# Score matmuls of the second block: from three passes of 64 rows for each head to one of 128 rows and one of 64

## The chip, the cores and the metric

The kernel runs on one core of a Trainium2 chip, as one launch. The metric is the device time of that launch in microseconds (us). A core has a matrix engine (TensorE, in the rows PE, its weight loads PEld), VectorE (DVE), ScalarE (ACT), GpSimd (POOL) and a queue engine (SP), which run side by side and wait for one another by semaphores.

## The reference

The reference is a net of two blocks of two layers each, over 512 tokens of width 1024, all in float32. The first block (RWKV-7, latent attention, a convolution, attention into a memory) is not touched. The second block is, for each layer:

```python
u = rmsnorm(h, attn_norm[l])
rq, rk, rv, rg, dq, dk, dv = split(u @ w_in[l])
# retention, 4 heads, q and k of 64: scores with a decay, causal
s = einsum('bnchd,bnshd->bnhcs', q, k) * decay
ret = silu(rg) * rmsnorm(retention(rq, rk, rv), ret_norm[l])
# differential attention, 4 heads, two q and two k of 64 each
s = einsum('bqhjd,bkhjd->bhjqk', qb, kb) * scale - slope * dist   # causal
p = softmax(s)
a = p[:, :, 0] - lam * p[:, :, 1]
dif = rmsnorm(a @ v, diff_norm[l]) * (1 - lam_init)
h = h + concat([ret, dif]) @ w_out[l]
h = h + (silu(u2 @ w_gate[l]) * (u2 @ w_up[l])) @ w_down[l]       # u2 = rmsnorm(h, ffn_norm[l])
```

What counts here are the two products of q and k, whose inner dimension is 64.

## The kernel before

Float32 products are made out of three passes in a rounded format (F32R): an operand x is split into hi, its rounding, and lo = x - hi, and a.b is taken as hi.hi + hi.lo + lo.hi, summed in PSUM. `hilo` (L259) makes the two parts: a ScalarE cast for hi (L260), a VectorE subtraction for lo (L243 by way of `tt`). Weights go the same way, from a raw tile `wr` to `wh` and `wl`. A projection (`proj`, L351) is 24 matmuls of 512 columns into a PSUM tile `pmm` (lines 289, 290 and 295), of which there are three; score tiles are `pat`, also three; `prw` two. SBUF tiles of the second block are K4 (18 of 4 KB per partition) and K2 (32 of 2 KB); all show as `K` in the rows.

Queries and keys come out of the projection transposed: 128 partitions by 512 tokens. The 128 partitions are two heads of 64 in retention, and in diff attention the two q (or k) of one head. `mm3_pair` (L274) makes the scores for both halves: for each of the three passes it issues one matmul on partitions 0 to 63 and one on 64 to 127, each into its own PSUM tile, with 64 rows of the array each. All its matmuls have the line L279.

`retention(l)` (L1416) projects rq and rk of two pairs of heads (p = 0, 1), multiplies each by a table of decays (L1427) and splits it (L1428). Its `scores(p)` goes over key blocks j in the groups (0), (1, 3), (2): the scores of keys j against the queries from 128 j on, so 512, 384, 128 and 256 columns; VectorE multiplies each by a mask out of PSUM (L1448), and `hilo` splits that. `diff(l)` (L1482) makes for each of four heads a `query(h)` (dq and dk projections, operands hi and lo in one K4 tile for q and one for k), then `scores(h)`: for query blocks i = 0 to 3 `attn_scores2` (L1026) makes the scores against 128 (i + 1) keys for both halves, and `attn_row` (L1035) reads them out of PSUM (L1037, bias and row maximum), then exponential, sum and so on. The order of emission is query(0), scores(0), query(1), scores(1), query(2), out(0), and so on: `out(h)` transposes the weights and multiplies by the values.

The order on each engine is set when the program is built: a planner takes the operation with the best priority (about the order of emission, shifted by `prio`) out of those that it reckons to be ready. On the chip each engine then follows its list in order. So a matmul whose operand is late holds up all that stand behind it on TensorE.

Of the kernel before, what the change touches and what calls it, by code (L numbers as in the profile page):

```python
# [12 lines left out]
F32 = mybir.dt.float32  # L13
F32R = mybir.dt.float32r
I32 = mybir.dt.int32
AF = mybir.ActivationFunctionType
ALU = mybir.AluOpType
# [193 lines left out]
class Net:  # L211
# [59 lines left out]
        mm(out, ah, bl, start=False, stop=False)  # L271
        mm(out, al, bh, start=False, stop=stop)  # L272

    def mm3_pair(self, ops):  # L274

        mm = self.nc.tensor.matmul
        for i in range(3):
            for out, ah, al, bh, bl in ops:
                mm(out, (ah, ah, al)[i], (bh, bl, bh)[i], start=(i == 0), stop=(i == 2))  # L279

    def mmset(self, out, terms, start=True, stop=True):

# [743 lines left out]
    def attn_scores2(self, Svs, q, k, i, bias):  # L1026

        with self.prio("attn_scores"):
            n = (i + 1) * 128
            pss = [self.PS("at") for _ in range(2)]  # L1030
            self.mm3_pair([(pss[j][:, 0:n], q[r, 0, ts(i, 128)], q[r, 1, ts(i, 128)], k[r, 0, 0:n], k[r, 1, 0:n])
                           for j, r in enumerate((slice(0, 64), slice(64, 128)))])
            return [self.attn_row(Svs[j], pss[j], n, bias, 1.0) for j in range(2)]

    def attn_row(self, Sv, ps, n, bias, sc):  # L1035
# [380 lines left out]
    def retention(self, l):  # L1416
        nc = self.nc
        tri = [self.T("K2") for _ in range(2)]
        for i in range(2):
            nc.gpsimd.dma_start(out=tri[i], in_=self.a["cstb"][8 + i])  # L1420
        qk = []
        for p in range(2):
            for i, nm in enumerate(("rq", "rk")):
                tab = self.T("K2")
                nc.gpsimd.dma_start(out=tab, in_=self.a["cstb"][2 * i + p])
                ps = self.proj(self.bchunk(l, nm, p) if p else self.early[i], cut=0 if p else 256)
                self.tt(tab, ps, tab, ALU.mult)  # L1427
                qk.append(self.split(tab))  # L1428
                yield

        def scores(p):

            (qh, ql), (kh, kl) = qk[2 * p:2 * p + 2]
            rows = [slice(64 * hh, 64 * hh + 64) for hh in range(2)]
            HL = [(self.T("K4", dt=F32R), self.T("K4", dt=F32R), self.T("K2", dt=F32R)) for _ in range(2)]
            ST = [[None] * 4 for _ in range(2)]
            for gi, grp in enumerate(((0,), (1, 3), (2,))):
                pss = [self.PS("at") for _ in range(2)]
                o = 0
                for j in grp:  # L1440
                    n = 512 - 128 * j
                    self.mm3_pair([(pss[hh][:, o:o + n], kh[r, ts(j, 128)], kl[r, ts(j, 128)], qh[r, 128 * j:512],
                                    ql[r, 128 * j:512]) for hh, r in enumerate(rows)])
                    o += n
                for hh in range(2):
                    H, Lo, M = HL[hh]
                    t = self.T("K2")
                    self.tt(t[:, 0:o], pss[hh][:, 0:o], tri[gi % 2][:, 0:o], ALU.mult)  # L1448
                    a, b = (H[:, ts(gi, 512)], Lo[:, ts(gi, 512)]) if gi < 2 else (M[:, 0:256], M[:, 256:512])
                    self.hilo(a, b, t[:, 0:o])  # L1450
                    i = 0
                    for j in grp:
                        n = 512 - 128 * j
                        ST[hh][j] = (a[:, i:i + n], b[:, i:i + n])
                        i += n
            return ST

        STs = scores(0)
        yield
        for h in range(4):  # L1460
            gt = self.silu2(self.proj(self.bchunk(l, "rg", h)))
            yield
            if h == 0:
                STs += scores(1)
            yield
            ST = STs[h]
            ps = self.PS("rw")
            for j in range(4):
                self.mm3(ps[:, 128 * j:512], self.vals[j][0][:, ts(h, 128)], self.vals[j][1][:, ts(h, 128)],
                         ST[j][0], ST[j][1], j == 0, j == 3)  # L1470
            y = self.rms_head(ps, self.bpar[:, l:l + 1])
            self.stt(y, y, 0.5, gt, ALU.mult, ALU.mult)
            self.dump("ret", y, h)
            self.mix_in(y)
            yield
# [6 lines left out]
    def diff(self, l):  # L1482
        nc = self.nc
        lam_init = 0.8 - 0.6 * math.exp(-0.3 * l)
        lt = self.T("K2", [128, 4, 64])
        nc.sync.dma_start(out=lt, in_=self.a["lam"][l].unsqueeze(0).broadcast_to([128, 4, 64]))
        st = self.tiny(4)
        for i in range(2):
            nc.vector.tensor_tensor_reduce(lt[:, 2 * i, :], lt[:, 2 * i, :], lt[:, 2 * i + 1, :], 1.0, 0.0,
                                           op0=ALU.mult, op1=ALU.add, accum_out=st[:, i:i + 1])  # L1490
        self.act(st[:, 0:2], st[:, 0:2], AF.Exp)
        self.tt(st[:, 2:3], st[:, 1:2], st[:, 0:1], ALU.subtract)
        nlam = self.tiny(2)
        self.tsc(nlam[:, 0:1], st[:, 2:3], -lam_init, ALU.add)
        self.tsc(nlam[:, 1:2], self.bpar[:, 2 + l:3 + l], 1.0 - lam_init, ALU.mult)
        yield
        def query(h):
            al = self.T("K2")
            nc.gpsimd.dma_start(out=al, in_=self.a["cstb"][4 + h])
            ps = self.proj(self.bchunk(l, "dq", h))  # L1500
            q, k = self.T("K4", [128, 2, 512], F32R), self.T("K4", [128, 2, 512], F32R)
            self.act(q[:, 0, :], ps, AF.Copy, scale=0.125)
            self.stt(q[:, 1, :], ps, 0.125, q[:, 0, :].bitcast(F32), ALU.mult, ALU.subtract)
            yield
            self.hilo(k[:, 0, :], k[:, 1, :], self.proj(self.bchunk(l, "dk", h)))
            yield
            qs[h] = al, q, k

        def scores(h):
            al, q, k = qs.pop(h)  # L1510
            Sj = [self.score_tiles() for _ in range(2)]
            for i in range(4):
                m0, m1 = self.attn_scores2([P[i] for P in Sj], q, k, i, al)
                self.tt(m1[:, 3:4], m1[:, 3:4], nlam[:, 0:1], ALU.mult)
                self.ptsc(Sj[1][i], Sj[1][i], m1[:, 3:4], ALU.mult, 1.0, ALU.mult)
                self.stt(Sj[0][i], Sj[0][i], m0[:, 3:4], Sj[1][i], ALU.mult, ALU.add)
            return Sj[0]

        def out(h, P):
            PT = self.attn_T(P)  # L1520
            ps = self.PS("rw")
            for j in range(4):
                self.mm3(ps[:, 128 * j:512], self.dvals[j][0][:, ts(h, 128)], self.dvals[j][1][:, ts(h, 128)],
                         PT[j][0], PT[j][1], j == 0, j == 3)
            y = self.rms_head(ps, nlam[:, 1:2])
            self.dump("dif", y, h)
            self.mix_in(y)

        qs = {}
        yield from query(0)  # L1530
        prev = None
        for h in range(4):
            P = scores(h)
            yield
            if h < 3:
                yield from query(h + 1)
            if prev:
                out(h - 1, prev)
                yield
            prev = P  # L1540
        out(3, prev)
        yield
# [165 lines left out]
```

## Time and profile before

| | |
|---|---|
| median of 3 runs | 2924.97 us (2923.43 to 2925.59) |
| the profiled execution's own time | 2923.72 us |
| its span, first to last instruction | 2921.9 us |
| mean granted clock of TensorE | 0.987 |
| TensorE / VectorE / ScalarE / GpSimd busy, share of the span | 97% / 60% / 39% / 10% |

A row of the timeline merges neighbouring instructions of one line on one engine: its first number is the start from the beginning of the span, the second how long the merged run lasts. Matmuls are pipelined, so that the next one starts before the one before it has ended; what a matmul costs TensorE is seen from start to start. In the rows `64*128 64x512` means that 64 rows and 128 columns of the array are used and that 512 columns stream through, and a bracket at the end gives the idle time before and what ended it.

### The profile page before, as it was taken

What the parts mean: (1) busy time and instruction counts of PE and PEld (TensorE: products, weight loads), DVE (VectorE), ACT (ScalarE), POOL (GpSimd) and SP (SyncE); (2) the same over time, 40 slices, a digit from 0 to 9 for tenths busy, and PEclk for the clock granted to TensorE, in tenths of its full rate; (3) what the DMA queues carried; (4) which work ended last, traced back from release to release, by engine and by line L of the source; (5) the groups of instructions that cost most, each with busy time, mean ns of one, the idle gap of its engine ahead of it and who ended that gap; (6) DMA issues with size and microseconds to landing.
All of it is one profiled execution on the core that took longest, in us unless ns stands there. A gap on an engine that the chain in (4) does not pass through costs nothing. (4 is left out here: it accounts for less than half of the span.)

```text
span 2921.9 us, 40859 instructions
## 1 busy us (share of the span) xinstructions
PE 2825.3 (97%) x15172; PEld 2305.8 (79%) x15172; DVE 1741.8 (60%) x3499; ACT 1154.0 (39%) x2230; POOL 298.3 (10%) x451
## 2 busy tenths in 40 slices
PE   8999989999999999989899999999999999999998
PEld 7777867777787878777687778788888887788888
DVE  7969467576669696485676645554433546544423
ACT  5445443343434455433433334433323335433322
POOL 0011021111001011111210101100000101100000
PEclk9999999999999999999999999999999999999999
DMA  5222223123342222231242232223333222233332
GB/s 172 73 76 67 79 76 93 44 81 117 106 141 80 74 67 73 78 87 57 74 136 66 87 98 81 73 84 97 105 97 106 88 66 81 73 94 101 101 94 91
DMA packets 134535, 258.09 MB, mean 88 GB/s; under 512 B 15936, under 2 KB 19776, under 8 KB 134336
## 3 DMA queue, kind: packets, MB, share of 16 engines
q1 hardware_dynamic: 128896, 239.22, 26.8%
q0 software_dynamic: 5440, 16.26, 2.1%
q8 instruction: 119, 1.95, 0.3%
q14 instruction: 80, 0.66, 0.1%
HBM read 248.60 MB, written 6.82 MB: 87 GB/s over the span
## 5 line engine op out<-in xcount | busy, mean ns | idle before, releaser
L243 DVE TENSOR_TENSOR wl<-wr,wh 128x512 fp32r<-128x512 f32 x792 | 541.1, 686 | 724.4 <-ACT wh L260 393.5
L289 PE MATMUL pmm<-xh,wh 128*128 128x512 f32 x2272 | 883.6, 391 | 1.5 <-DVE K L243 1.5
L290 PE MATMUL pmm<-xl,wh 128*128 128x512 f32 x2272 | 878.6, 389 | 0.0
L260 ACT CAST wh<-wr 128x512 fp32r<-128x512 f32 x792 | 487.5, 616 | 848.3 <-PE pmm L290 528.6
L295 PE MATMUL pmm<-xh,wl 128*128 128x512 f32 x2272 | 578.6, 391 | 0.0
L289 PEld LDWEIGHTS pmm<-xh,wh 128*128 128x128 f32 x2272 | 429.1, 189 | 88.1 <-PE pmm L295 2.3
L290 PEld LDWEIGHTS pmm<-xl,wh 128*128 128x128 f32 x2272 | 428.8, 189 | 85.1 <-issue 0.8
L295 PEld LDWEIGHTS pmm<-xh,wl 128*128 128x128 f32 x2272 | 420.0, 190 | 85.8 <-issue 2.8
L246 DVE SCALAR_TENSOR_TENSOR cacc<-hp,par,cacc 128x512 f32<-128x512 f32 x240 | 183.1, 763 | 4.1
L243 DVE TENSOR_TENSOR K<-K,K 128x512 fp32r<-128x512 f32 (+14 forms) x261 | 151.1, 583 | 57.4 <-ACT K L260 49.9
L260 ACT CAST K<-K 128x512 fp32r<-128x512 f32 (+1 forms) x122 | 73.5, 606 | 186.2 <-DVE K L246 129.8
L289 PE MATMUL pmm<-K,wh 128*128 128x512 f32 (+1 forms) x352 | 135.1, 392 | 5.1 <-DVE big L246 4.0
L254 POOL TENSOR_SCALAR K<-K,tiny 128x256 f32<-128x256 f32 (+3 forms) x128 | 80.4, 635 | 505.3 <-DVE tiny L250 221.1
L290 PE MATMUL pmm<-K,wh 128*128 128x512 f32 (+1 forms) x352 | 131.2, 380 | 0.0
L422 PE MATMUL pat<-cst,K 128*128 128x128 f32 (+2 forms) x656 | 102.2, 277 | 21.0 <-DVE K L246 13.0
L240 ACT ACTIVATE K<-pmm 128x512 f32<-128x512 f32 (+1 forms) x118 | 70.6, 598 | 108.6 <-PE pmm L295 108.5
L257 POOL TENSOR_TENSOR tiny<-tiny,negh 128x4 f32<-128x4 f32 (+2 forms) x54 | 66.0, 1222 | 454.6 <-DVE tiny L251 280.2
L422 PEld LDWEIGHTS pat<-cst,K 128*128 128x128 f32 (+2 forms) x656 | 76.8, 141 | 35.5 <-DVE K L246 10.6
L270 PE MATMUL pmm<-wh,K 128*128 128x512 f32 x260 | 103.8, 402 | 0.0
L272 PE MATMUL pmm<-wh,K 128*128 128x512 f32 x260 | 103.6, 398 | 0.0
L271 PE MATMUL pmm<-wl,K 128*128 128x512 f32 x260 | 103.6, 398 | 0.0
L246 DVE SCALAR_TENSOR_TENSOR K<-K,pmm 128x512 f32<-128x512 f32 x130 | 88.4, 680 | 5.9 <-ACT K L240 5.9
(335 smaller groups left out, 4132.6 us busy)
## 6 DMA issues: line engine op xcount, KB each, us to landing
wr<-in_wA SPq DMA_DIRECT2D x316, 256.0 KB, 2.7
wr<-in_wgu SPq DMA_DIRECT2D x176, 256.0 KB, 2.9
wr<-in_wo SPq DMA_DIRECT2D x64, 256.0 KB, 2.8
wr<-in_wout SPq DMA_DIRECT2D x64, 256.0 KB, 2.9
wr<-in_wB SPq DMA_DIRECT2D x64, 256.0 KB, 2.8
wr<-in_wdA SPq DMA_DIRECT2D x44, 256.0 KB, 2.8
wr<-in_wdB SPq DMA_DIRECT2D x44, 256.0 KB, 2.7
K<-in_cstb POOLq DMA_DIRECT2D x20, 256.0 KB, 3.3
```

Source lines behind the costliest of these rows:

```text
L240: return self.nc.scalar.activation(out, in_, func, bias=bias, scale=scale, **kw)
L243: return self.nc.vector.tensor_tensor(out=out, in0=a, in1=b, op=op)
L246: return self.nc.vector.scalar_tensor_tensor(out=out, in0=a, scalar=s, in1=b, op0=op0, op1=op1)
L254: return self.nc.gpsimd.tensor_scalar(out=out, in0=a, scalar1=s1, scalar2=s2, op0=op0, op1=op1)
L260: self.nc.scalar.copy(h, src)
L270: mm(out, ah, bh, start=start, stop=False)
L271: mm(out, ah, bl, start=False, stop=False)
L272: mm(out, al, bh, start=False, stop=stop)
L289: mm(out, ah, bh, start=start and i == 0, stop=False)
L290: mm(out, ah, bl, start=False, stop=False)
L295: mm(out, al, bh, start=False, stop=stop and i == n - 1)
L422: self.nc.tensor.transpose(out, in_, self.ident[b:b + k, :k] if k == 128 else self.ident[b:b + k, b:b + k])
```

## The change

Of the two operands of a score product, one is stacked and the other doubled. For a half (64 partitions), the stacked operand holds hi in its own 64 partitions and lo in the other 64 of one tile; the doubled operand holds hi in both. One pass of 128 rows then gives hi.hi + lo.hi. A second pass, of 64 rows, multiplies the stacked tile's hi part by the doubled operand's lo, which has a tile of its own. So each half has two passes instead of three, and they are issued half by half: full, half, full, half. In retention q is doubled and k is stacked, in diff q is stacked and k doubled. The parts are made by operations over 64 partitions each. Other users of `hilo` and `mm3` stay as they are.

```diff
-    def mm3_pair(self, ops):
-
-        mm = self.nc.tensor.matmul
-        for i in range(3):
-            for out, ah, al, bh, bl in ops:
-                mm(out, (ah, ah, al)[i], (bh, bl, bh)[i], start=(i == 0), stop=(i == 2))
+    def stacked(self, a, b, src, scale=None):
+
+        for t, r, o in ((a, slice(0, 64), slice(64, 128)), (b, slice(64, 128), slice(0, 64))):
+            if scale is None:
+                self.nc.scalar.copy(t[r, :], src[r, :])
+                self.tt(t[o, :], src[r, :], t[r, :].bitcast(F32), ALU.subtract)
+            else:
+                self.act(t[r, :], src[r, :], AF.Copy, scale=scale)
+                self.stt(t[o, :], src[r, :], scale, t[r, :].bitcast(F32), ALU.mult, ALU.subtract)
+        return a, b
+
+    def doubled(self, a, b, lo, src):
+
+        for t, r, o in ((a, slice(0, 64), slice(64, 128)), (b, slice(64, 128), slice(0, 64))):
+            self.nc.scalar.copy(t[r, :], src[r, :])
+            self.nc.scalar.copy(t[o, :], src[r, :])
+            self.tt(lo[r, :], src[r, :], t[r, :].bitcast(F32), ALU.subtract)
+        return a, b, lo
+
+    def mm_half(self, out, half, st, db, q, n0, n1):
+
+        r = slice(64 * half, 64 * half + 64)
+        self.nc.tensor.matmul(out, st[half][:, q], db[half][:, n0:n1], start=True, stop=False)
+        self.nc.tensor.matmul(out, st[half][r, q], db[2][r, n0:n1], start=False, stop=True)
...
-            self.mm3_pair([(pss[j][:, 0:n], q[r, 0, ts(i, 128)], q[r, 1, ts(i, 128)], k[r, 0, 0:n], k[r, 1, 0:n])
-                           for j, r in enumerate((slice(0, 64), slice(64, 128)))])
+            for j in range(2):
+                self.mm_half(pss[j][:, 0:n], j, q, k, ts(i, 128), 0, n)
...
-                qk.append(self.split(tab))
+                t = [self.T("K2", dt=F32R) for _ in range(2 + (i == 0))]
+                qk.append(self.stacked(*t, tab) if i else self.doubled(*t, tab))
...
-                    self.mm3_pair([(pss[hh][:, o:o + n], kh[r, ts(j, 128)], kl[r, ts(j, 128)], qh[r, 128 * j:512],
-                                    ql[r, 128 * j:512]) for hh, r in enumerate(rows)])
+                    for hh in range(2):
+                        self.mm_half(pss[hh][:, o:o + n], hh, ks, qd, ts(j, 128), 128 * j, 512)
...
-            self.act(q[:, 0, :], ps, AF.Copy, scale=0.125)
-            self.stt(q[:, 1, :], ps, 0.125, q[:, 0, :].bitcast(F32), ALU.mult, ALU.subtract)
-            yield
-            self.hilo(k[:, 0, :], k[:, 1, :], self.proj(self.bchunk(l, "dk", h)))
+            q = self.stacked(q[:, 0, :], q[:, 1, :], ps, 0.125)
+            yield
+            k = self.doubled(k[:, 0, :], k[:, 1, :], self.T("K2", dt=F32R), self.proj(self.bchunk(l, "dk", h)))
```

## Rows read from the trace of the kernel before

**Rows 1.** The page: TensorE's busy time, share of the span, instructions.

```profile
PE 2825.3 (97%) x15172; PEld 2305.8 (79%) x15172; DVE 1741.8 (60%) x3499; ACT 1154.0 (39%) x2230; POOL 298.3 (10%) x451
```

**Rows 2.** Busy time by stage, a stretch with a diff head; ends with granted clock, DMA.

```profile
1791.00:1807.00 16.00, 15.78 (x78) 12.61 (x76) 10.94 (x41) 7.75 (x19) 0.00 (x0) 1.00 0.34 106
```

**Rows 3.** Timeline of TensorE, 0.05 us at the first retention scores.

```profile
1695.94 0.39 PE L295 MATMUL pmm<-xh,wl 128*128 128x512 f32 x1
1696.26 0.51 PE L279 MATMUL pat<-K,K 64*128 64x512 f32 x2
```

**Rows 4.** Timeline of TensorE, a single score matmul among those of 128 rows.

```profile
1711.09 0.50 PE L279 MATMUL pat<-K,K 64*128 64x512 f32 x1
1711.51 0.50 PE L290 MATMUL pmm<-K,xh 128*128 128x512 f32 x1
1711.85 0.40 PE L289 MATMUL pmm<-K,xh 128*128 128x512 f32 x1
1712.08 0.40 PE L290 MATMUL pmm<-K,xh 128*128 128x512 f32 x1
```

**Rows 5.** Timeline of TensorE, matmuls of 384, 256 and 128 columns.

```profile
1835.66 0.33 PE L270 MATMUL prw<-K,K 128*128 128x384 f32 x1
...
1836.19 0.28 PE L270 MATMUL prw<-K,K 128*128 128x256 f32 x1
...
1836.54 0.22 PE L270 MATMUL prw<-K,K 128*128 128x128 f32 x1
...
1836.71 0.27 PE L272 MATMUL prw<-K,K 128*128 128x128 f32 x1
1836.92 0.95 PE L279 MATMUL pat<-K,K 64*128 64x128 f32 x9
```

**Rows 6.** Timeline of TensorE, runs of score matmuls of the first layer.

```profile
1696.26 1.79 PE L279 MATMUL pat<-K,K 64*128 64x512 f32 x12
1699.10 1.81 PE L279 MATMUL pat<-K,K 64*128 64x384 f32 x12 [1.04 <-DVE K L243]
1701.58 1.61 PE L279 MATMUL pat<-K,K 64*128 64x512 f32 x3 [0.68 <-DVE K L243]
1703.12 1.65 PE L289 MATMUL pmm<-K,xh 128*128 128x512 f32 x3
...
1734.65 1.07 PE L279 MATMUL pat<-K,K 64*128 64x512 f32 x7
...
1736.76 1.81 PE L279 MATMUL pat<-K,K 64*128 64x384 f32 x12
...
1803.15 4.19 PE L279 MATMUL pat<-K,K 64*128 64x128 f32 x24
1807.27 0.50 PE L289 MATMUL pmm<-xh,wh 128*128 128x512 f32 x1
...
1842.12 2.83 PE L279 MATMUL pat<-K,K 64*128 64x256 f32 x15
```

**Rows 7.** Granted clock by stretch: length, TensorE busy, clock, DMA share, GB/s.

```profile
1701.30:1708.10 6.80, 6.52 (x15) 0.50 0.39 117
2322.50:2329.30 6.80, 6.47 (x15) 0.50 0.34 114
```

**Rows 8.** Timeline of TensorE, projection at the lower clock.

```profile
1704.57 0.63 PE L290 MATMUL pmm<-K,xh 128*128 128x512 f32 x1
1704.99 0.63 PE L289 MATMUL pmm<-K,xh 128*128 128x512 f32 x1
```

**Rows 9.** Timeline of VectorE at the first retention scores.

```profile
1697.75 0.69 DVE L243 TENSOR_TENSOR K<-K,K 128x512 fp32r<-128x512 f32 x1 [0.69 <-ACT K L260]
1698.36 1.88 DVE L243 TENSOR_TENSOR K<-pat,K 128x512 f32<-128x512 f32 x3
```

**Rows 10.** Groups by shape, operations over 64 partitions: busy time, mean ns.

```profile
L260 ACT CAST K<-pmm 64x512 fp32r<-64x512 f32 x16 | 9.3, 581 | 0.2
L243 DVE TENSOR_TENSOR K<-pmm,K 64x512 fp32r<-64x512 f32 x16 | 10.9, 684 | 0.8 <-ACT K L260 0.7
```

More of the change, by code (lines that the diff above doesn't have):

```diff
@@ L1427, in retention @@
                 self.tt(tab, ps, tab, ALU.mult)
-                qk.append(self.split(tab))
+                t = [self.T("K2", dt=F32R) for _ in range(2 + (i == 0))]
+                qk.append(self.stacked(*t, tab) if i else self.doubled(*t, tab))
                 yield
         def scores(p):
-            (qh, ql), (kh, kl) = qk[2 * p:2 * p + 2]
-            rows = [slice(64 * hh, 64 * hh + 64) for hh in range(2)]
+            qd, ks = qk[2 * p:2 * p + 2]
             HL = [(self.T("K4", dt=F32R), self.T("K4", dt=F32R), self.T("K2", dt=F32R)) for _ in range(2)]
```

## The prediction, made before the changed kernel was run

> **What bounds the kernel now.** I read the page first: TensorE holds 97% of the span [rows 1], so a time on TensorE counts in full unless it takes the place of a wait. Busy time there is the union of pipelined matmuls and hides small gaps, so the sums below go by start times from the timeline of TensorE alone. The table of stages shows what the change's other engines have left around a head of diff attention [rows 2]: VectorE is busy 10.94 of 16 us, ScalarE 7.75. Neither is the bound; VectorE has the less to spare.
>
> The question is then what the score matmuls of line 279 cost TensorE. Three things are to be seen.
>
> First, the two heads of a pair already share the array. Two matmuls of 64 rows and 512 columns start within 0.05 us of each other and together last 0.51 us [rows 3]; one alone lasts 0.50 us [rows 4]. So three passes over two heads can cost about three passes, not six.
>
> Second, going between 64 and 128 rows costs time. In the steady run the matmuls of 512 columns start 0.23 us apart (1711.85 to 1712.08). Around the single score matmul at 1711.09 the next starts come after 0.42 and 0.34 us [rows 4]; a matmul of 64 rows comes 0.32 us after the start of 128 rows before it (1695.94 to 1696.26) [rows 3]. So one matmul of 64 rows among those of 128 takes 0.32 + 0.42 + 0.34 = 1.08 us where three steady starts take 0.69: 0.40 us for two switches, 0.20 each. About 0.09 of that comes before the new matmul starts, and about 0.11 after, where its weights have to be loaded before it streams (0.50 us long against 0.39 to 0.40).
>
> Third, the pairs run far from their best, since they wait. A head of diff attention has 24 matmuls, which hold TensorE from 1803.15 to 1807.27, 4.12 us [rows 6]; twelve perfect pairs would need half of that. In retention there are idle stretches of 1.04 and 0.68 us ended by VectorE [rows 6], and then a granted clock of 0.50, the 1.2 GHz level, from 1701.3 to 1708.1, and the same in the second layer from 2322.5 [rows 7].
>
> **The old cost.** Diff, one layer: two heads run as 24 in a row, 4.12 us each; the other two run as 9 and 15, rows of 0.95 and 2.83 us [rows 5, 6], whose last 0.07 us lies under the next matmul (4.19 against 4.12 for the run of 24), so 0.88 + 2.76 = 3.64 us. From start to next start a run already holds its own weight load and the drain at its end; 0.09 before it and 0.11 in the next matmul come on top, 0.20 a run: 2 x 4.32 + 2 x (3.64 + 0.40) = 16.7 us. Retention, one layer: 1696.26 to 1703.12 is 6.86; the two singles (the second is shown in [rows 4]) take 0.42 each; the runs of 7 and 12 take 1.00 and 1.74; five runs pay 0.20: 11.4 us. Two layers: 33.4 + 22.9 = 56.3 us. Beside it the half clock: from 1703.12 to 1708.1 projection matmuls start 0.42 us apart (1704.57 to 1704.99) [rows 8] instead of 0.23, so 5.0 us lose 5.0 x (1 - 0.23/0.42) = 2.3 us, 4.6 in two layers.
>
> **The new cost on TensorE.** For each of 12 units (8 diff heads, 4 retention pairs) there are four widths, 128, 256, 384 and 512 columns, and two heads, and for each of these one pass of 128 rows and one of 64: 16 matmuls where there were 24. The order in mm_half is full, half, full, half, so every matmul switches. From the values' matmuls [rows 5] a steady pass takes 0.23 us for 512 columns, 0.177 for 384 (three in 0.53), 0.117 for 256 (three in 0.35) and 0.085 for 128 (two in 0.17): 0.61, times four 2.44 us. Sixteen switches at 0.20 add 3.2: 5.64 us a unit, 67.7 us for twelve. That the switch costs the narrow passes as much as the wide is seen at 1836.92, where a run of 64 rows enters 0.21 us after a start of 128 columns, against 0.085 without a switch [rows 5]. Diff: 8 x 5.64 = 45.1 against 33.4, **+11.7 us**. Retention: 4 x 5.64 = 22.6 against 22.9, and its first unit also waits for VectorE (below), 0.5 us in each layer: **+0.7 us**.
>
> Here a rule speaks against the change: the Trainium skill, in "TensorEngine Tiling (Array Packing)", Tiling Modes, says that changing the tiling mode drains the engine. In "TensorE: Matmul & The Clock Gate", Part 3, it says that a weight load passes running matmuls only where the row group differs, but names a background weight buffer too. By the first of these the 0.11 us stays at each switch and the sum stands; by a buffer that also covers a change of rows it goes, and the sum falls by 192 x 0.11 = 21 us. The 0.42 and 0.34 us in [rows 4] agree with the former.
>
> **Clock.** In retention the idle 1.04 us goes: TensorE has 5.6 us of its own to do there. I take the two falls of the clock as gone, **-4.6 us**; the bounds are 0 (the alternating passes bring them as the waits did) and -4.6.
>
> **Operands.** A unit's hi and lo of q and k took two ScalarE and two VectorE operations over 128 partitions. stacked takes two and two, doubled four and two. An operation on 64 partitions is not cheaper: 581 ns and 684 ns [rows 10]. So each unit adds four on ScalarE (2.3 us) and two on VectorE (1.4 us), 28 and 16 us in all. In the stage of [rows 2], a head in some 16 us, VectorE goes from 0.68 to about 0.77: covered, as is the longer hold of the projection's PSUM tile, which has two more buffers, each a cover of 24 matmuls at 0.23 (5.5 us). Without that cover the 16 us would count. What is exposed is the start of a unit: the first full pass needs two copies where one did, the second head's four. For each diff head that is 0 (the planner fills that place with whatever is ready, and can put more there) to 0.68 us (one VectorE operation): 0 to 5.4 us; I take **+2**, since the fill exists for three heads of four. In retention VectorE's queue does rk's product, waits for ScalarE's cast, subtracts (1697.75), and only then reads the first scores (1698.36) [rows 9]. stacked puts one more subtraction (0.6 us between starts) before that read, and through three score buffers in PSUM it delays the fourth of the six groups; that is the 0.5 us above. The extra 2 KB tile per unit has 32 buffers: nothing, or a late weight of w_out at worst. No DMA is added or moved.
>
> **Sum.** +11.7 + 0.7 - 4.6 + 2 = +9.8 us. With the waits at nothing it is +7.8; with them in full and both falls of the clock left, +17.8. The profiled execution took 2923.7 us (span 2921.9), 1.3 below the median of the runs, so this gives 2933.5 on its own scale; I say **2933 us**, own range 2928 to 2941, chance 0.52.
>
> **Rivals.**
> *The weights load behind the stream (faster).* In a regular alternation the next weights might be loaded while the last pass still streams, so that a switch costs 0.09. Then a unit takes 2.44 + 16 x 0.09 = 3.88 us, 46.6 for twelve against 56.3: -9.7, then +1.0 for VectorE in retention, -4.6 for the clock and +2 for the waits: -11.3, 2912. It decides below about 0.15 us a switch, where the sum crosses zero (9.8/192 = 0.05 less). Against it: the intervals of [rows 3, 4]. Chance 0.12.
> *The waits took it anyway (no change).* Half of the old 4.12 us was waiting for tiles and operands. If the new passes fit more of those waits, and the tails where the heads end on softmax hide the rest, half of diff's +11.7 goes: +4.0, 2928. For it: the waits in [rows 6] are VectorE's. Against: 3.2 us of switches is work that nothing hides. Chance 0.24.
> *The clock falls with every head (much slower).* The clock fell once after score matmuls that waited [rows 6, 7]; passes that alternate might do the same, in every unit. At 2.3 us a fall, eight diff heads give +18, half of them +9: 2942 to 2952. Against: the clock was 1.00 in the stretch of [rows 2], which holds most of such a run, and projection fills the sides. Chance 0.12.
>
> **How the numbers follow.** 0.2%, 5.9 us, is about what a measurement tells from no change. The forecast's case is slower by more than that in 0.45 and same in 0.07; the waits' case same in 0.20, slower in 0.04; the clock's slower in 0.12; the weights' faster in 0.11, same in 0.01. Slower 0.61, same 0.28, faster 0.11. The range 2920 to 2946 leaves out most of the faster rival (0.10) and the worst of the clock's (0.06).
>
> **What the profile would show.** Line 279 gone, 192 matmuls in its place, alternating 128 and 64 rows, starts 0.42 us apart at 512 columns and 0.26 to 0.30 at 128: the switch is right. Starts near 0.32 would prove the faster rival. A clock of 1.00 around 1701 would confirm that term; 0.50 after diff heads the third rival. TensorE waits for ScalarE's cast before a unit would size the exposed copies. The prediction is wrong if the planner splits the passes so that halves of two heads lie side by side, or if the weights of values or w_out come late.

## The result, and the profile after

| | before | after |
|---|---|---|
| median of the runs | 2924.42 us (4 runs, 2923.43 to 2925.59) | 2945.69 us (4 runs, 2942.49 to 2950.49) |
| profiled execution, span | 2923.72, 2921.9 us | 2950.49, 2948.7 us |
| mean granted clock of that execution | 0.987 | 0.982 |

The changed kernel is slower: ratio 1.0077, 95% interval 1.0058 to 1.0097, or +21 us. The forecast was +8 to +10. The sign was right and the time lies inside the range, at its upper end, but the size was off by more than twice.

First the page of the changed kernel (each engine's busy time, share of the span, instructions), as in [rows 1]:

```profile
PE 2853.6 (97%) x15076; PEld 2312.2 (78%) x15076; DVE 1762.6 (60%) x3523; ACT 1182.2 (40%) x2278; POOL 297.3 (10%) x451
```

TensorE has 96 matmuls fewer (288 gone, 192 new) and is busy 28 us longer. That is the whole of the longer span: nothing else became the bound. ScalarE is up by 28.2 us and VectorE by 20.8, near the 28 and 16 that the prediction counted.

Next the timeline of TensorE (start, duration, both us) in a diff head with projection beside it. Line 296 is the pass of 128 rows, line 297 that of 64:

```profile
1854.19 0.28 PE L296 MATMUL pat<-K,K 128*128 128x256 f32 x1
1854.40 0.38 PE L297 MATMUL pat<-K,K 64*128 64x256 f32 x1
1854.71 0.44 PE L296 MATMUL pat<-K,K 128*128 128x384 f32 x1
1855.08 0.44 PE L297 MATMUL pat<-K,K 64*128 64x384 f32 x1
1855.45 0.50 PE L307 MATMUL pmm<-xh,wh 128*128 128x512 f32 x1
1855.79 0.33 PE L296 MATMUL pat<-K,K 128*128 128x384 f32 x1
1856.05 0.44 PE L297 MATMUL pat<-K,K 64*128 64x384 f32 x1
1856.42 0.49 PE L296 MATMUL pat<-K,K 128*128 128x512 f32 x1
1856.84 0.50 PE L297 MATMUL pat<-K,K 64*128 64x512 f32 x1
1857.27 0.50 PE L308 MATMUL pmm<-xl,wh 128*128 128x512 f32 x1
```

The rows alternate, as forecast. From a pass to the next that has other rows it takes 0.42 or 0.43 us at 512 columns (1856.42 to 1856.84 to 1857.27), 0.37 at 384, 0.31 at 256; the 128-column passes below start 0.25 to 0.26 apart. The four make 0.43 + 0.37 + 0.31 + 0.255 = 1.365, a unit of sixteen passes 5.46 us; the prediction had 5.64. Where a pass of 128 rows follows a projection matmul of 128 rows (1855.45 to 1855.79), nothing is lost beyond that matmul's own late start: 0.34, as in [rows 4]. The pass of 64 rows after it then comes sooner, too (0.26 at 384 columns, 1855.79 to 1856.05).

The rows of the weight loads show where the price lies. The load of a pass that changes rows starts only with the pass itself:

```profile
1856.42 0.19 PEld L296 LDWEIGHTS pat<-K,K 128*128 128x128 f32 x1 [0.19 <-DVE tiny L1059]
1856.84 0.18 PEld L297 LDWEIGHTS pat<-K,K 64*128 64x128 f32 x1 [0.24 <-issue]
```

Now retention, which waited in [rows 6]. The timeline of TensorE from the last passes before the wait on:

```profile
1703.87 0.33 PE L296 MATMUL pat<-K,K 128*128 128x128 f32 x1
1704.12 0.32 PE L297 MATMUL pat<-K,K 64*128 64x128 f32 x1
1704.38 0.44 PE L296 MATMUL pat<-K,K 128*128 128x384 f32 x1
...
1705.37 0.32 PE L297 MATMUL pat<-K,K 64*128 64x128 f32 x1
1706.76 0.39 PE L296 MATMUL pat<-K,K 128*128 128x256 f32 x1 [1.07 <-DVE K L243]
1707.08 0.58 PE L297 MATMUL pat<-K,K 64*128 64x256 f32 x1
```

The wait of 1.04 us on VectorE has not gone. It comes one score tile later, is 1.07 us long, and has the same end: VectorE's multiplication that reads the scores out. Before, twelve matmuls made the first three tiles of the unit, and the fourth waited; now twelve passes make four, and the fifth waits, with all three score buffers in use. The timeline of VectorE says why: between its reading of the first score tile and of the second lie three operations over 64 partitions.

```profile
1703.21 0.68 DVE L243 TENSOR_TENSOR K<-pat,K 128x512 f32<-128x512 f32 x1
1703.98 2.13 DVE L243 TENSOR_TENSOR K<-K,K 64x512 fp32r<-64x512 f32 x3
1706.02 0.68 DVE L243 TENSOR_TENSOR K<-pat,K 128x512 f32<-128x512 f32 x1
```

From the second pass after the wait on, the matmuls run at the lower clock, as the table of stretches says (length, busy time of TensorE, its weight loads, VectorE, ScalarE and GpSimd with their counts, granted clock, DMA share, GB/s). Its first and fifth rows answer to [rows 7]:

```profile
1707.00:1713.80 6.80, 6.80 (x15) 4.40 (x15) 6.17 (x13) 4.39 (x9) 1.61 (x3) 0.50 0.34 107
...
1826.00:1842.00 16.00, 15.55 (x62) 10.57 (x61) 12.60 (x49) 9.81 (x25) 3.06 (x5) 1.00 0.26 82
...
1874.30:1884.50 10.20, 9.45 (x22) 5.44 (x23) 6.32 (x32) 4.11 (x14) 2.13 (x4) 0.50 0.00 0
1894.80:1898.20 3.40, 3.40 (x11) 2.72 (x10) 1.98 (x3) 1.58 (x3) 0.00 (x0) 0.50 0.00 0
2341.90:2348.70 6.80, 6.80 (x15) 4.54 (x15) 6.16 (x12) 4.08 (x9) 1.61 (x3) 0.50 0.37 116
...
2509.20:2519.40 10.20, 9.72 (x23) 5.61 (x24) 6.25 (x33) 4.00 (x14) 1.87 (x4) 0.50 0.00 0
```

Retention keeps its 6.8 us at half clock in either layer, exactly as before. Heads with projection beside them keep the full clock: the second row, with VectorE at 0.79 (12.60 of 16 us; the prediction said 0.77). At the fourth diff head each layer has 10.2 us at half clock, and 3.4 us more some 20 us after that begins. The profile before has 6.8 us from 2482.9 on and 3.4 later in the second layer, with the old passes, and nothing in the first, where the last head ran at the full clock, with more than twice the matmuls of the change's stretch in the same time:

```profile
2482.90:2489.70 6.80, 6.80 (x23) 5.08 (x22) 5.45 (x30) 3.21 (x10) 1.44 (x3) 0.50 0.00 1
...
1860.00:1870.00 10.00, 9.72 (x53) 7.07 (x54) 8.12 (x36) 6.36 (x20) 1.69 (x5) 1.00 0.00 1
```

What is different about the fourth head is in the timeline. There is no projection of a next head to put between the passes; the matmuls of the values and of w_out (lines 270 to 272) and the small ones of the third head's normalization (L464, L486) are all there is:

```profile
1875.05 0.69 PE L486 MATMUL prw<-cst,tiny 128*128 128x128 f32 x2 [0.80 <-POOL tiny L257]
1875.39 0.56 PE L296 MATMUL pat<-K,K 128*128 128x256 f32 x1
1875.88 0.58 PE L297 MATMUL pat<-K,K 64*128 64x256 f32 x1
1876.39 0.69 PE L296 MATMUL pat<-K,K 128*128 128x384 f32 x1
1877.01 0.69 PE L297 MATMUL pat<-K,K 64*128 64x384 f32 x1
1877.63 0.47 PE L486 MATMUL prw<-cst,tiny 128*128 128x128 f32 x1
```

At the lower clock a pass of 384 columns takes 0.62 us to the next where it took 0.37. In the 5 us before the fall TensorE had run the values' matmuls, three pairs of passes of 128 and 256 columns, eight matmuls of one column and four of w_out; the fall comes with the start of the 0.80 us for which it waits for GpSimd.

By start times of the same work, after minus before: retention +1.8 and +0.9 us in the two layers, diff attention with w_out +11.3 and +7.3, together +21.3 in the stretches that the change touches. The other 5 us of the profiled difference were there before the first score matmul: 1696.26 against 1701.53 us. They vary from one execution to another; in e11 below it starts at 1692.54.

### The profile page after: what moved, and what is told of

Its sections match the earlier page's. It is cut to its first block, busy times and chain, and to the rows that moved or that the text cites. A ratio compares the mean times of both kernels' runs of the same rounds, so it can differ in the third digit from the quotient of the medians.

```text
span 2948.7 us, 40734 instructions
## 1 busy us (share of the span) xinstructions
PE 2853.6 (97%) x15076; PEld 2312.2 (78%) x15076; DVE 1762.6 (60%) x3523; ACT 1182.2 (40%) x2278; POOL 297.3 (10%) x451
## 4 chain that ended last, share of the span: by engine, by line
PE 43%; DVE 4%; DMA 2%; ACT 1%; POOL 1%; issue 1%; DVEq 0%; POOLq 0%; ACTq 0%
PE pmm L313 9%; PE pmm L307 9%; PE pmm L308 9%; PE pmm L272 2%; PE pmm L270 2%; PE pmm L271 2%; DVE K L243 1%; PE pat L297 1%; PE pat L271 1%; PE pat L270 1%; PE pat L272 1%; DVE K L246 1%; PE pat L296 1%; PE prw L270 1%; PE prw L271 1%
## 5 line engine op out<-in xcount | busy, mean ns | idle before, releaser
L243 DVE TENSOR_TENSOR K<-K,K 128x512 fp32r<-128x512 f32 (+15 forms) x269 | 155.9, 583 | 61.6 <-ACT K L260 45.3
L440 PE MATMUL pat<-cst,K 128*128 128x128 f32 (+2 forms) x656 | 103.0, 277 | 20.5 <-DVE K L246 12.6
L240 ACT ACTIVATE K<-pmm 128x512 f32<-128x512 f32 (+2 forms) x126 | 75.3, 598 | 107.1 <-PE pmm L313 104.1
L440 PEld LDWEIGHTS pat<-cst,K 128*128 128x128 f32 (+2 forms) x656 | 77.5, 141 | 33.6 <-DVE K L246 11.7
```

What stands on the lines that cost most here:

```text
L240: return self.nc.scalar.activation(out, in_, func, bias=bias, scale=scale, **kw)
L243: return self.nc.vector.tensor_tensor(out=out, in0=a, in1=b, op=op)
L440: self.nc.tensor.transpose(out, in_, self.ident[b:b + k, :k] if k == 128 else self.ident[b:b + k, b:b + k])
```

## The experiments

Two theories stood after this. **Switches and clock:** the passes cost what they were priced at, and the alternation at the fourth head, which has no projection beside it, brings the clock down. **Late operands:** the six extra ScalarE and VectorE operations on the way to the first pass of a unit make TensorE wait, and the clock falls on the waits. All results stand in one table. A ratio is to the kernel before, run in the same session on the same chip. "Half clock" is from each profile, diff attention with w_out in both layers, in stretches of 1.7 us: twice the part of the clock that is missing, times 1.7, summed. The last two columns split the mean over all runs, less that of 72 runs of the kernel before (2922.5 us at a mean clock of 0.9867). Each run lists its granted clock, and over some 170 runs of 13 kernels, with a constant for each kernel, 0.001 of it goes with 2.53 us. What the clock doesn't account for is the rest.

| kernel | ratio, 95% interval | half clock, us | mean clock | clock part + rest, us |
|---|---|---|---|---|
| before | 1 | 10.2 | 0.9867 | 0 |
| the change | 1.0077 [1.0058, 1.0097] | 27.3 | 0.9830 | 9.2 + 14.4 |
| e9_change_again | 1.0057 [1.0036, 1.0079] | 6.8 | 0.9853 | 3.3 + 15.6 |
| e1_operands_only | 1.0023 [1.0005, 1.0042] | 17.1 | 0.9853 | 3.4 + 5.9 |
| e2_grouped | 1.0063 [1.0040, 1.0085] | 23.9 | 0.9842 | 6.1 + 13.0 |
| e3_no_switch | 0.9954 [0.9938, 0.9969] | 3.4 | 0.9892 | -6.4 - 7.3 |
| e4_heads_0_to_2 | 1.0015 [1.0001, 1.0030] | 0.0 | 0.9878 | -2.9 + 6.8 |
| e5_head_3_only | 1.0033 [1.0015, 1.0050] | 20.4 | 0.9849 | 4.4 + 4.0 |
| e6_retention_only | 1.0004 [0.9989, 1.0020] | 13.6 | 0.9864 | 0.6 - 1.2 |
| e7_head_3_no_switch | 1.0037 [1.0026, 1.0048] | 6.8 | 0.9876 | -2.4 + 10.4 |
| e8_head_3_old_passes | 1.0038 [1.0025, 1.0052] | 6.8 | 0.9870 | -0.9 + 10.5 |
| e10_diff_only | 1.0052 [1.0034, 1.0071] | 27.4 | 0.9853 | 3.5 + 13.1 |
| e11_no_switch_gpsimd | 0.9957 [0.9941, 0.9972] | 3.4 | 0.9888 | -5.3 - 4.8 |

**e1_operands_only: the new operand operations, the old passes.** The operands are made by as many operations per half as in the change, and the old paired passes read them; the doubled copy goes to a tile that nothing reads. The edit is to the kernel before.

```diff
+    def parts(self, h, l, src, scale=None, extra=None):
...
+        for r, o in ((slice(0, 64), slice(64, 128)), (slice(64, 128), slice(0, 64))):
+            if scale is None:
+                self.nc.scalar.copy(h[r, :], src[r, :])
+                if extra is not None:
+                    self.nc.scalar.copy(extra[o, :], src[r, :])
+                self.tt(l[r, :], src[r, :], h[r, :].bitcast(F32), ALU.subtract)
...
-                qk.append(self.split(tab))
+                t = [self.T("K2", dt=F32R) for _ in range(2 + (i == 0))]
+                qk.append(self.parts(t[0], t[1], tab, None, None if i else t[2]))
...
+            self.parts(q[:, 0, :], q[:, 1, :], ps, 0.125)
+            yield
+            self.parts(k[:, 0, :], k[:, 1, :], self.proj(self.bchunk(l, "dk", h)), None, self.T("K2", dt=F32R))
```

> The operands are made by as many operations over 64 partitions as in the change (six casts or copies on ScalarE and four subtractions on VectorE for a pair of q and k; the extra copies go to a tile that nothing reads), but the scores are the old three passes of 64 rows, two halves side by side. Theory A (the switches between 64 and 128 rows on TensorE and the falls of its clock cost the 21 us): 0 to +4 us against the kernel before, ratio 1.000 to 1.0014. Theory B (the added 28 us of ScalarE and 16 us of VectorE hold up the scores, and with them TensorE): +10 to +21 us, ratio 1.0035 to 1.007.

Measured 2929.35 us against 2922.03, +7.3, between the two ranges expected. The operands alone cost 5.9 us beside the clock, so they are a part of the slowdown, and the smaller one. This is about the prediction's upper bound (5.4), not the +2 that was taken.

**e2_grouped: both heads' passes of 128 rows, then both of 64.** Half the switches, as the code is written.

```diff
+        for h in range(2):
+            mm(outs[h], st[h][:, q], db[h][:, n0:n1], start=True, stop=False)
+        for h in range(2):
+            r = slice(64 * h, 64 * h + 64)
+            mm(outs[h], st[h][r, q], db[2][r, n0:n1], start=False, stop=True)
```

> The operands and passes of the change in another order: both passes of 128 rows first, then the two of 64 rows, which lie on different rows of the array. A unit then has 8 switches instead of 16, and the two half passes can share the array: 3/4 of 2.44 us and 8 x 0.20 are 3.4 us where the change takes 5.5 and the kernel before 4.0 to 4.5. Theory A: 12 x 2.1 = 25 us below the change if the clock falls go too, so -4 us against the kernel before, between -12 and +4. Theory B: the operands are as before this order, so within 5 us of the changed kernel, +16 to +21 us.

Measured 2941.65 us, no better than the change, but the timeline of TensorE in this kernel shows why that tells nothing (line 297 is the pass of 128 rows, line 300 that of 64):

```profile
1825.79 0.34 PE L297 MATMUL pat<-K,K 128*128 128x384 f32 x1
1826.06 0.43 PE L300 MATMUL pat<-K,K 64*128 64x384 f32 x1
1826.42 0.44 PE L297 MATMUL pat<-K,K 128*128 128x384 f32 x1
1826.80 0.44 PE L300 MATMUL pat<-K,K 64*128 64x384 f32 x1
```

The planner has issued most of them in the old alternation: of the 96 passes of 128 rows, 12 have another of 128 as the next score pass (4 in the change). The experiment is inconclusive on grouping; it does show that the order of the source is not the order of issue.

**e3_no_switch: the second pass takes 128 rows too.** The remainder lies in one tile per head, whose other half GpSimd fills with zeros; the rows added multiply zeros.

```diff
+        los = [lo, self.T("K2", dt=F32R)]
...
+            self.nc.gpsimd.memset(l[o, :].bitcast(F32), 0.0)
...
-        self.nc.tensor.matmul(out, st[half][r, q], db[2][r, n0:n1], start=False, stop=True)
+        self.nc.tensor.matmul(out, st[half][:, q], db[2][half][:, n0:n1], start=False, stop=True)
```

> As the change, but the second pass has 128 rows too: the lo of the doubled operand has a tile for each half, whose other 64 partitions GpSimd fills with zeros. Four passes of 128 rows and no switch: 2.44 us a unit against 5.5. Theory A: 12 x 3 = 37 us below the change and the clock at its upper level beside the scores, so -12 us against the kernel before, between -20 and -4. Theory B: +16 us or more, since all operations of the change are there and GpSimd's come on top.

Measured 2909.53 us against 2922.03: 12.5 us faster than the kernel before, and by the ratios some 30 to 36 faster than the change, with the same number of matmuls. The timeline of TensorE in a diff head (both passes are of 128 rows now):

```profile
1820.69 0.39 PE L297 MATMUL pat<-K,K 128*128 128x512 f32 x1
1820.92 0.40 PE L298 MATMUL pat<-K,K 128*128 128x512 f32 x1
1821.15 0.40 PE L297 MATMUL pat<-K,K 128*128 128x512 f32 x1
1821.39 0.40 PE L298 MATMUL pat<-K,K 128*128 128x512 f32 x1
```

and the weight loads of the second and third of these passes, which start with the pass before:

```profile
1820.69 0.19 PEld L298 LDWEIGHTS pat<-K,K 128*128 128x128 f32 x1
1820.94 0.19 PEld L297 LDWEIGHTS pat<-K,K 128*128 128x128 f32 x1
```

The passes start 0.23 us apart where they started 0.42 apart. So the 0.20 us belongs to the change of rows, not to the number of passes, nor to their operands, and it is about the time of one load (0.18 to 0.19 us) that no longer lies behind the stream. Here a rule of the Trainium skill can be measured: "TensorEngine Tiling (Array Packing)", Tiling Modes, says that a change of mode drains TensorE. The trace agrees: here a change costs 0.17 us at 128 columns to 0.20 at 512.

Not all of it comes back as time. 192 switches at 0.19 us are 36 us, the rest column falls by 22 to 23 from the change to e3, and the other part of the gain is the clock's. TensorE waits more in e3: in the first layer its score passes wait 3.7 us for VectorE, up to 2.0 at a time, where the change's wait 1.5.

**e4_heads_0_to_2, e5_head_3_only, e6_retention_only: the change in parts.** The rest of each kernel keeps the old operands and passes.

```diff
+            if h in (0, 1, 2):      # e4; (3,) in e5; () in e6
+                q = self.stacked(...)
+                yield
+                k = self.doubled(...)
+            else:
+                q, k = (q[:, 0, :], q[:, 1, :]), (k[:, 0, :], k[:, 1, :])
+                self.act(q[0], ps, AF.Copy, scale=0.125)
+                self.stt(q[1], ps, 0.125, q[0].bitcast(F32), ALU.mult, ALU.subtract)
+                yield
+                self.hilo(k[0], k[1], self.proj(self.bchunk(l, "dk", h)))
...
                 qk.append(self.split(tab))      # e4 and e5, as before; e6 has the change's line
```

> Only heads 0 to 2 of diff attention, which have projections beside them, use the new passes; head 3 and retention are as before. Theory A in its first form (the switches alone): 6 heads x 1.3 us = +7.5 us. Theory A with the clock (of the 21 us some 9 are falls of the clock at the last head, and not here): +5 to +9 us too, and no new stretch at the lower clock beside heads 0 to 2. If each head cost the same share of the 21 us, operands or not, it would be 6 of 12 units: +10.6 us.

> Only head 3 of diff attention, the last, which has no projection of a next head beside it, uses the new passes; the rest is as before. In the runs so far 0.001 of mean granted clock goes with 2.6 us, and by that the change's 22.8 us (means) are 8.8 of clock and 13.9 of other time. If the clock falls beside the last head (theory A): clock lower by 0.002 to 0.003, +5 to +8 us, and +2.5 us for the passes of two heads: +8 to +11 us in all. If the falls come from retention (rival C): +2 to +4 us and the clock as before.

> Only retention uses the new passes; diff attention is as before. Theory A: retention's own sum was +0.7 us, and its two old falls of the clock stay: 0 to +3 us, clock as before. Rival C (the new falls are retention's): clock lower by 0.002 to 0.003, +6 to +9 us. The prediction's term (retention's falls vanish) would give -4 us and a clock higher by 0.0015.

Measured 2925.16 us (e4, against 2922.03), 2929.77 (e5) and 2920.59 (e6, both against 2921.26). The +3.1 of e4 lies under the +5 to +9 expected. One head out of four costs over twice what the other three cost together. The stretches of e5 around the fourth head, in both layers:

```profile
1862.50:1872.70 10.20, 10.20 (x26) 6.43 (x26) 5.84 (x30) 3.21 (x10) 1.45 (x3) 0.50 0.00 0
2487.10:2497.30 10.20, 10.20 (x26) 6.24 (x26) 6.09 (x30) 3.21 (x10) 1.45 (x3) 0.50 0.00 1
```

These are the falls of the changed kernel, at the same place and of the same length, with three heads and retention left as they were. In the profile of e4 no fall is left in this stage, although its fourth head is that of the kernel before, which had 10.2 us. Retention alone is neutral: the granted clock there is not bought back, nor is more of it lost. In e6 the fourth head has the old operands and passes, and the clock falls there as well, in both layers, for 6.8 us; this is the first:

```profile
1863.00:1869.80 6.80, 6.80 (x28) 5.58 (x28) 5.81 (x30) 3.22 (x10) 1.44 (x3) 0.50 0.00 0
```

So the alternation is not what it takes for a fall at this head. What it changes, as far as these profiles go, is how long and how often the clock falls there.

**e7_head_3_no_switch, e8_head_3_old_passes: the change, with other passes at the fourth head.** In e7 its second pass takes 128 rows, as in e3; in e8 it has the old paired passes, but as many operand operations as the change.

```diff
+            if h == 3:              # e7
+                los = [self.T("K2", dt=F32R) for _ in range(2)]
+                k = self.doubled0(k[:, 0, :], k[:, 1, :], los, self.proj(...))
...
+            if h < 3:               # e8
...
+            else:
+                q = self.parts(q[:, 0, :], q[:, 1, :], ps, 0.125)
+                yield
+                k = self.parts(k[:, 0, :], k[:, 1, :], self.proj(...), None, self.T("K2", dt=F32R))
```

> The change, but in head 3 the second pass has 128 rows too (its lo in two tiles with zeros in the other half). Operands and their times are those of the change, only the switches of that head go. If the switching passes let the clock fall there (theory A): clock up by about 0.003 against the change, and 2 x 3 us less in passes: 12 to 15 us below the change, so +7 to +10 us against the kernel before. If late operands let it fall (rival D): only the 6 us of passes go, +15 to +17 us.

> The change, but head 3 has the old three passes of pairs, with as many operations for its operands as in the change. Theory A: the passes are what lets the clock fall, so clock up by about 0.003 against the change: +10 to +13 us against the kernel before. Rival D (the operands come late at the last head and TensorE waits): the clock stays where the change has it, +18 to +21 us.

Measured 2930.32 and 2932.41 us, both against 2921.26: 9 to 11 us over the kernel before, where the change is 18 to 21. Their mean clocks, 0.9876 and 0.9870, are those of the kernel before. The stretches around the fourth head in e8, in both layers:

```profile
1875.00:1885.00 10.00, 9.59 (x52) 7.17 (x52) 8.49 (x37) 6.49 (x18) 2.14 (x4) 1.00 0.00 0
2500.30:2507.10 6.80, 6.80 (x28) 5.33 (x27) 5.22 (x28) 3.31 (x11) 1.44 (x3) 0.50 0.01 2
```

In the first layer VectorE and ScalarE do more than in the change (8.49 and 6.49 us in 10), TensorE waits the same 0.80 us for GpSimd ahead of these passes, and the clock stays at the upper level. In the second, after the same wait, it falls for 6.8 us, as in the kernel before and in e6. The mean clocks of the twelve runs, not these stretches, are what speaks against late operands at this head and for the passes.

**e9_change_again: the changed kernel once more, nothing edited.** It went with e10 and e11, to see how far executions of one kernel differ.

> The changed kernel once more, beside the next two on one chip. Its parts so far, each against the kernel before (means): heads 0 to 2 +4.4, head 3 +8.9, retention -0.2, together +13 us, while the change itself had +24 by means of 4 runs. If the first figure of the change was high by chance of the clock, this one is nearer to +13, with a clock of 0.985; if the parts do more together than alone, +20 to +24 and 0.983.

Measured 2941.5 us (six runs, 2932.17 to 2950.75) against 2923.29: +18 us. Its profiled execution is the fastest of the six, 2932.17 us, within 1 us of the forecast. Span and mean granted clock of that one, and then of the first profile of the same code:

```profile
core 0: 2930.4 us, clock 0.988
```

```profile
core 0: 2948.7 us, clock 0.982
```

In it the alternation at the fourth head ran at the upper clock; 3.4 us at half clock came only some 12 us after the last of these passes, in either layer. This is the timeline of TensorE there:

```profile
1868.27 0.45 PE L296 MATMUL pat<-K,K 128*128 128x384 f32 x1
1868.64 0.44 PE L297 MATMUL pat<-K,K 64*128 64x384 f32 x1
```

So the long fall at the fourth head is likely and not certain. A mean of 0.982 over 2948.7 us is 2 x 0.018 x 2948.7 = 106 us at half clock, 0.988 over 2930.4 us is 70. At 0.43 us for each (2.53 us for 0.001 of the clock, which is 5.85 us at half of it) the 36 us between them are worth 15 of the 18.3 us between the spans. Summed over stretches of 1.7 us, the difference is 37.6 us: 20.5 in diff attention with w_out, 3.4 in retention, and 13.7 in stages that the change does not touch.

The six runs, +18 us at a mean clock of 0.9853, lie between the two cases expected.

**e10_diff_only: all four diff heads changed, retention as before.**

```diff
+            if h in (0, 1, 2, 3):   # as e4, with the fourth head
```

> All four heads of diff attention have the new passes, retention is as before. Retention alone changed nothing, so if the parts do more together it is heads 0 to 2 with head 3: as the change itself, +20 to +24 us. If they simply add: +13 us. If it is retention's changed time that pushes something over: +13 us here and +20 in the change.

Measured 2938.69 us against 2923.29, +15.4, with 13.7 us at half clock in diff attention in each layer, as in the change. Most of the slowdown is there, between the +13 and the +20 to +24 expected; the change itself, in the same session, is 3 us higher, and the intervals overlap.

**e11_no_switch_gpsimd: e3, with the doubled copy on GpSimd.**

```diff
-            self.nc.scalar.copy(t[o, :], src[r, :])
+            self.ptsc(t[o, :], t[r, :].bitcast(F32), 1.0, ALU.mult, 1.0, ALU.mult)
```

> The version without switches (both passes of 128 rows), with the second copy of the doubled operand moved from ScalarE to GpSimd, which takes it from the first copy in SBUF. If the added ScalarE work is what the operands cost (the operands alone had +5.8 us beside the clock), it is 3 to 6 us faster than the version without switches: -15 to -19 us against the kernel before. If GpSimd's copy, with 1.2 us after the cast instead of 0.6, comes too late, or the VectorE work is the cost: -8 to -13 us.

Measured 2910.63 us against 2923.29, ratio 0.9957: the same as e3 within the intervals. ScalarE's second copy is not what is left over in e3.

## Why the prediction was right in sign and short in size

**The price of a switch held.** 0.20 us from the two places of [rows 3, 4] gave a unit of 5.64 us; the trace gives 5.46. The faster rival, in which weights load behind the stream, is out: where 512-column passes alternate without a break they start 0.42 to 0.43 us apart. Starts 0.32 apart, its sign, do occur, but only at a pass of 128 rows that follows another matmul of 128 and so has its weights already, and the next start then comes after 0.43. e3 shows how much hung on it.

**The sum without the clock held, with two errors that cancel.** Passes, retention and operands were put at 11.7 + 0.7 + 2 = 14.4 us; the rest column gives 14.4 and 15.6 for the changed kernel. Within it the operands cost 5.9 us (e1), not 2, which leaves 8 to 10 for the passes, not 12.4, if the two simply add. That the errors cancel is luck. In which waits the operands' 5.9 us lie was not settled; the cover that was claimed for three heads of four did not hide them. The rival in which waits take half of the passes' cost is not borne out in the sum, since such a kernel would have had a rest near 9; but the 3 to 4 us that the passes fell short of their price, and what e3 did not give back, say that waits took a part.

**The step that failed is the clock: -4.6 us taken, +3.3 to +9.2 measured.** It failed in two ways. First, the falls in retention were taken as gone because the wait of 1.04 us would go. The prediction itself had VectorE reading the scores later, through three score buffers, and priced that at 0.5 us, but did not ask where the rest of the wait would then be: at the fifth score tile, 1.07 us long. Both falls stayed, so this term was 0. Every one of the thirteen profiles has 3.4 to 10.2 us at half clock in retention of each layer, whatever the passes are. Second, the price of new falls was bounded at nothing, and left to the third rival. That rival's mechanism is the one that happened, at one head of four: e4 shows no fall at the heads that have projection beside them, e5 shows long ones at the fourth alone, and the mean clocks of e7 and e8 are back at that of the kernel before. The view of [rows 2], on which the prediction rested its clock of 1.00, holds a head with projection on both sides. The head without it was in the same trace and wasn't asked about, and "the clock fell once" is not what that trace shows: it has 6.8 us at half clock beside the fourth head of the second layer, with the old passes.

In the two profiled executions the sum closes with this term. At 0.43 us for each, the 13.6 and 3.4 us more at half clock in diff attention of the two layers are 5.9 and 1.5 of the 11.3 and 7.3 us by start times. That leaves 5.4 and 5.8 for passes and operands, with retention's 1.8 and 0.9 together 13.9 us, against 14.4 in the sum; the clock gave +7.4 where -4.6 was taken.

How strong is this? For retention the profiles are plain. At the fourth head and in w_out, the five kernels with the old passes there (before, e1, e4, e6, e8) have 0 to 17.1 us at half clock, 9.5 in the mean; the five that alternate there (the change, its repeat, e2, e5, e10) have 6.8 to 27.4, 21.2 in the mean; the three with 128 rows throughout (e3, e7, e11) 3.4 to 6.8. Each figure is one execution, and the ranges overlap: the alternation makes the falls longer and more frequent, and why one execution falls and the next does not stays open. The means over all runs point the same way. The five kernels whose fourth head alternates (the change, its repeat, e2, e5, e10) have mean clocks of 0.9830 to 0.9853, the six others with edited heads or retention 0.9864 to 0.9892. e1 is the exception, 0.9853 with the old passes, and so late operands at all units may lower the clock as well; e8 speaks against them for the fourth head alone. Single profiles differ a great deal, as e9 shows, and a mean clock is that of the whole execution: before the first score matmul, where no kernel was edited, the thirteen profiles have 31 to 61 us at half clock. The Trainium skill, in "TensorE: Matmul & The Clock Gate", "A second HAM failure mode: psum-queue depth-cycling", describes a kernel whose clock swings between its levels although TensorE pauses only shortly between groups of matmuls. Of this the trace shows the low clock beside short pauses, 10.2 us at 0.50 with TensorE busy for 9.45 of them; no run here shows what makes it fall.

**What stays open.** The parts do not add up to the whole: e4, e5 and e6 give 3.9 + 8.4 - 0.6 = 11.7 us in the means, the change 18.9 and 23.6, e10 without retention 16.6. In the rest column it is 9.6 against 14.4 and 15.6. Either new heads 0 to 2 make the fourth worse (its start is later, and so is what stands beside it), or a few us of it are the spread of the means. No run tells these apart.

## What to carry to other kernels

Price the change of row count between neighbouring matmuls before the number of passes: twelve units of sixteen passes that alternate between 128 and 64 rows lost to the old pairs, and the same passes padded with zeros to 128 rows beat both (0.9954). Ask for the granted clock of the barest place that an edit touches, the last head with nothing to run beside it, not of a typical one. And when a wait is said to go, follow the resource behind it to the next instruction that needs it: with three buffers it moved from the fourth score tile to the fifth and kept its length.

## What the runs showed of the hardware that was not expected

- A matmul whose weights take 0.19 us to load can start 0.23 us after one of the same 128 rows (e3): its load starts with the matmul before. Only between 64 and 128 rows is the load bare.
- The kernel before, unedited, took 2911.5 to 2937.0 us in 72 runs, at mean granted clocks of 0.982 to 0.991. A time of it is to be read with its clock beside it.
- Passes that keep 128 rows gained clock as well: 0.9892 (e3) and 0.9888 (e11) against 0.9867, some 6 of the 10 to 14 us.
